# Small matmuls of a chunked recurrence issued in unbroken runs, with regrouped low-rank and first projections, in a two-layer decoder step on one core

## The chip, the core and the metric

The program runs on one core of a Trainium2 chip. The core has a matmul engine (TensorE, PE in the profile, with its weight loads shown as PEld), VectorE (DVE), ScalarE (ACT), GpSimd (POOL) and a queue for transfers (SP). Each engine takes its instructions in the order in which the program lists them. The metric is the device time of one execution in microseconds (us), the median of several runs.

## The reference

One inference step over two layers, for 1040 prompt tokens (16 learned ones ahead of 1024 given ones) and 8 single decode tokens, with width 1024. Layer 0 has a causal convolution module as its token mixer, layer 1 has RWKV-7 time mixing with 16 heads of 64; a squared-ReLU MLP of width 4096 follows each.

```python
def _wkv7_step(S, inp):                      # one token of the recurrence, per head
    r_t, w_t, k_t, v_t, kk_t, a_t = inp
    sa = jnp.einsum('bhvk,bhk->bhv', S, -kk_t)
    S = (S * w_t[:, :, None, :] + sa[..., None] * (kk_t * a_t)[:, :, None, :]
         + v_t[..., None] * k_t[:, :, None, :])
    y = jnp.einsum('bhvk,bhk->bhv', S, r_t)
    return S, y
...
    xx = prev - h                            # _rwkv7: six mixed inputs x? = h + xx * x_mix[?]
    r = (xr @ w_r).astype(f32)
    k = (xk @ w_k).astype(f32)
    v = (xv @ w_v).astype(f32)
    w_log = -jax.nn.softplus(-(w0 + jnp.tanh(xw @ w1) @ w2).astype(f32)) - 0.5
    decay = jnp.exp(-jnp.exp(w_log))
    a = jax.nn.sigmoid((a0 + (xa @ a1) @ a2).astype(f32))
    g = jax.nn.sigmoid(xg @ g1) @ g2
    kk = (k * k_k.astype(f32)).reshape(hs)
    kk = kk / jnp.maximum(jnp.sqrt(jnp.sum(kk * kk, axis=-1, keepdims=True)), L2_EPS)
    ...
    out = ((yn + bonus).astype(h.dtype) * g) @ w_o
```

## The kernel before

**Precision.** Every large product is three matmuls (`mm3`, L209 to L213): weight and activation are each split into a high and a low part (`_hi`/`_lo`, `_h`/`_l` or `mh`/`ml`), and high·high, low·high and high·low are summed in one PSUM bank. The splits are made by ACT (the high part, L177 or L159) and by POOL or DVE (the low part, L182 or L160).

**Stages in time.** Layer 0 runs first (three token groups of about 350). The mixer of layer 1 runs over four token groups of about 260 (`mixer_in(g)`); for each group it makes the eight `r` projections (`p_r`), the eight `k` projections (`p_k`) and the eight `v` projections (`p_v`), one per 128 output columns, each 24 matmuls. Before each of the three stands `mixed(i)`, which makes eight activation tiles (DVE L877, then the split). Beside them run the low-rank branches: `gate()` and `decay_rate()` call `narrow()`, 48 matmuls for one bank (`p_g`, `p_wa`), and the second stages `l_g`, `l_w`, `l_a` are three matmuls per 128 columns. The decay branch's result is split into `lwh`/`lwl` and `lah`/`lal`. `spread()` (`pb`, L804) spreads the key norms over the partitions, two matmuls into the one bank of pool `x`, read by DVE at L1157. `finish()` makes the blocks `nn` for the recurrence, sixteen matmuls of 64 x 32 per 128 columns. Last come the output projection (`ps_oo`) and the MLP of layer 1 (`ps_in`, `out`), for one token group and then for two.

**The recurrence** goes in 17 chunks of 64 tokens (`chunk(c)`), each prepared by `front(c)` (`A`, and the inverse of 32 x 32 blocks on DVE, L1232 and L1233). The chunk's products are small: `gg` and `po` are sixteen matmuls of 32 x 32 each, `W`, `U`, `S` sixteen of 64 columns each, `Y` 32. In the profile each of these shows as two records, as do all with f32 operands. They use only a part of the array (the profile prints the part, as 32\*32, 64\*64, 128\*64, 64\*32). One chunk is a chain: `W` needs the state `sv`; `U` needs `w1`, a copy of `W`, and `p64`, into which `po` is copied; `S` needs `uv`, a copy of `U`; the next state needs `S`.

**What sets the order.** The code is generators that a driver steps (`beside`, `filler`, `advance`), so that chunks, norm gates and MLP are traced interleaved. A list scheduler then orders each engine's instructions by readiness in its own estimate and by the place in the trace; `tc.high_priority(offset)` moves what it encloses up in that order. The eight banks of PSUM are shared in turn: in mixer groups 1 to 3, `mm` has four, `x` one and `w` (recurrence, transposes, `A`) three.

In the `r`, `k` and `v` stages the side generators are stepped by `beside(gen, places)`, at the calls whose number modulo 3 is in `places`.

Of the kernel before, what the change touches and what calls it, by code (L numbers as in the profile page):

```python
# [16 lines left out]
P = 128  # L17
# [31 lines left out]
def hybrid_step(tc, x_prompt, x_sample, state_conv, state_shift, state_wkv, meta_tokens,  # L49
# [10 lines left out]
    with ctx:  # L60
# [158 lines left out]
        def dense_steps(w, act, n, name):  # L219
            ps = bank(f"ps_{name}")  # L220
            for k in range(KT):
                mm3(ps[:, :n], (w[0][:, k, :], w[1][:, k, :]), (act[0][:, k, :n], act[1][:, k, :n]), k == 0, k == KT - 1)
                if k == KT // 2 - 1:
                    yield
            return ps
# [72 lines left out]
        def mlp_in(pl, hv, n, layer, name, sums):  # L298
# [3 lines left out]
            for k in range(KT):  # L302
                g = vec("norm_mlp", layer * KT + k)
                nc.scalar.activation(ah[:, k, :n], hv[:, k, :], AF.Copy, scale=g)  # L304
                nc.vector.scalar_tensor_tensor(al[:, k, :n], hv[:, k, :], g, ah[:, k, :n].bitcast(F32),
                                               op0=ALU.mult, op1=ALU.subtract)
# [25 lines left out]
        HEAD = 8  # L332
        STEPS = 2.6
# [80 lines left out]
        with ExitStack() as le:  # L414
# [76 lines left out]
            def transpose_x(g, ah, al):  # L491
# [19 lines left out]
                for k in range(KT):  # L511
# [4 lines left out]
                    nc.scalar.activation(ah[:, k, :n], ps[:, :n], AF.Copy, scale=gk)  # L516
                    nc.vector.scalar_tensor_tensor(al[:, k, :n], ps[:, :n], gk, ah[:, k, :n].bitcast(F32),
# [85 lines left out]
            def ln_silu(g):  # L603
# [14 lines left out]
                for k in range(KT):  # L618
# [4 lines left out]
                    split(ah[:, k, :n], al[:, k, :n], s[:, :n], nc.gpsimd)  # L623
# [208 lines left out]

        prep = {}
# [57 lines left out]
        def mixer_in(g, tick, ahead):  # L891
# [33 lines left out]

            nl = n if npr == n else npr + 2 * DEC
# [20 lines left out]
            def narrow(i, name):  # L947

                ps = bank(nm("p", name))[:, :nl]
                for hf in range(2):  # L950
                    w = load_w(d_lr[i, :, hf * HK:(hf + 1) * HK].rearrange("p k s c -> p (k s) c"), (KT, P), nm(name, hf), nc.gpsimd)
                    yield
                    for k in range(hf * HK, hf * HK + HK):
                        for s_ in range(2):
                            j = k % HK * 2 + s_
                            mm3(ps, (w[0][:, j, :], w[1][:, j, :]), [t[:, 1 - s_:1 - s_ + nl] for t in hxs[k]],
                                j == 0 and hf == 0, j == KT - 1 and hf == 1)
                        yield
# [15 lines left out]
            def gate():  # L974
                yield from input_parts()
# [31 lines left out]
            def beside(gen, places, slow=1.0):  # L1007
# [3 lines left out]
                def trace():  # L1011
                    tick(slow)
                    if calls[0] % 3 in places:
# [6 lines left out]
            aside = gate()  # L1020
            both = beside(aside, (0, 1))
            for p in range(KT):
                (both if p else lambda: tick(1.0))()
                ps = proj(next(wrkv), act, P, f"r{p}", both if p else lambda: tick(1.0))
                if p == 0:
                    carry["tail"]()
                r = t_("st", p, "em", 2)
# [42 lines left out]


            for _ in aside:
                pass
            act = mixed(3)
            both = beside(ahead, (1, 2), VSLOW)

            def finish(p, rk, ab, vv):
                def trace():
# [25 lines left out]
                    for c in range(ncg):  # L1104
                        for q in range(2):
                            for j in range(2):
                                o, js = 64 * q + 32 * j, slice(32 * j, 32 * j + 32)
                                nc.tensor.matmul(pn_[o:o + 32, c * 32:(c + 1) * 32], ab[HALF[q], c, 2, js], ab[HALF[q], c, 0, js],
                                                 start=True, stop=True, tile_position=(64 * q, o))
# [26 lines left out]
            for p, rk2 in ahead_of(fetch):  # L1136
# [18 lines left out]
                pb = bank(nm("pb", p), "x")  # L1155
# [140 lines left out]

        def chunk(c):
# [7 lines left out]
            def quads(name, pairs, lhs, rhs):  # L1305
                ps = bank(f"{name}{c}", "w")
                for p in range(KT):
                    for i, o in pairs:
                        nc.tensor.matmul(ps[Q[o], p * 32:(p + 1) * 32], lhs(i, p), rhs(i, p), start=True, stop=True,
                                         tile_position=(32 * i, 32 * o))  # L1310
                return ps, ps[:, :256].rearrange("p (k t) -> p k t", k=KT)
            down, up = [(0, 1), (2, 3)], [(1, 0), (3, 2)]

            ps, _ = quads("gg", down, lambda i, p: no[Q[i], p, :], lambda i, p: x32[Q[i], p, :])
            gg = w_([P, KT, 32], "gg", c, "x32")
            for i in (1, 3):
                nc.scalar.copy(flat(gg[Q[i]]), ps[Q[i], :256])
# [11 lines left out]
            for h in range(2):  # L1329
# [3 lines left out]
                nc.scalar.copy(flat(bkt[:, h * 4:h * 4 + 4]), ps)  # L1333
            yield RW[3]

            ps = bank(f"W{c}", "w")
            for p in range(KT):
                for q in range(2):
                    nc.tensor.matmul(ps[HALF[q], p * HS:(p + 1) * HS], xa[:, p, q, :HS], sv[:, p, q, :], start=True, stop=True)
# [371 lines left out]
```

## Time and profile before

| | us |
|---|---|
| median of 3 runs | 2870.38 (2868.0 to 2870.67) |
| the profiled execution | 2873.75 |
| its span, first to last instruction | 2872.0 |
| PE busy / PEld / DVE / ACT / POOL | 2708.4 / 2579.9 / 1986.7 / 1348.8 / 1627.1 |
| layer 0 alone, then beside the first mixer group | 0 to 898, 898 to 1245 |
| mixer groups 1 to 3 (with chunks 0 to 10) | 1245 to 1877 |
| output projection, first group, then MLP with chunks 12 to 16 | 1877 to 1924, 1924 to 2145 |
| rest of layer 1 | 2145 to 2872 |

A row of a view by windows gives a stretch, then for each engine its busy time and its number of instructions, then the granted PE clock (1.00 is full), the share of the transfer engines and GB/s. In a timeline a row has its start, its length, engine, line, operation, output and inputs, the part of the array, the size of the result and the number of records in a row. Matmuls are pipelined: the distance between two starts, not the length, is what one costs.

### The profile page before, as it was taken

The page shows a single profiled execution, that of the slowest core. Times are in us where ns is not written, and L with a number is a line of the kernel's source. Part 1 is how long each engine was busy: PE and PEld are TensorE (multiplying, and loading weights), DVE is VectorE, ACT ScalarE, POOL GpSimd, SP SyncE. Part 2 cuts the span into 40 slices and gives each one's busy share as a digit, 9 for nine tenths or more (in the row PEclk, how much of TensorE's full clock was granted, in tenths as well). Part 3 has the DMA queues.
Part 4 walks back from the last instruction along what each step waited for, and adds up shares of the span by engine and source line. Part 5 has one row for each costly group of instructions (what it writes and reads, how often), then busy time and mean ns, then how long its engine had stood idle before and what let it go on. Part 6 is the DMA issues. An engine that isn't in the chain of part 4 may idle for free. (4 is left out here: it accounts for less than half of the span.)

```text
span 2872.0 us, 54182 instructions
## 1 busy us (share of the span) xinstructions
PE 2708.4 (94%) x20554; PEld 2579.9 (90%) x20554; DVE 1986.7 (69%) x3752; ACT 1348.8 (47%) x2517; POOL 1627.1 (57%) x2191
## 2 busy tenths in 40 slices
PE   8999999999998999978888989989999999999998
PEld 7989999999998999978787778778789999999998
DVE  5999999995467455788886794674697664443444
ACT  5545444544354345555666755543344452222223
POOL 6687878987775454643444363454457783333332
PEclk9999999999999999989898989888999999999999
DMA  6572544454445555686778857865457642222211
GB/s 181 156 197 87 157 138 132 138 180 137 140 122 159 158 151 164 204 217 174 214 188 219 207 157 191 213 174 133 128 136 232 188 132 85 69 72 67 67 59 41
DMA packets 659283, 428.32 MB, mean 149 GB/s; under 512 B 126840, under 2 KB 609208, under 8 KB 659022
## 3 DMA queue, kind: packets, MB, share of 16 engines
q1 hardware_dynamic: 652780, 421.93, 52.4%
q8 instruction: 162, 2.65, 0.4%
q10 hardware_dynamic: 6018, 2.89, 0.4%
q14 instruction: 99, 0.81, 0.1%
q0 software_dynamic: 224, 0.03, 0.0%
HBM read 353.03 MB, written 72.66 MB: 148 GB/s over the span
## 5 line engine op out<-in xcount | busy, mean ns | idle before, releaser
L182 POOL TENSOR_TENSOR wo_lo<-wo_raw,wo_hi 128x256 fp32r<-128x256 f32 x672 | 517.1, 801 | 333.9 <-ACT wo_hi L177 287.5
L182 POOL TENSOR_TENSOR wi_lo<-wi_raw,wi_hi 128x256 fp32r<-128x256 f32 x600 | 462.7, 802 | 331.2 <-ACT wi_hi L177 318.3
L211 PE MATMUL out<-hh,wo_hi 128*128 128x352 f32 (+2 forms) x1536 | 503.7, 330 | 19.0 <-DVE h L382 8.2
L382 DVE TENSOR_TENSOR h<-h,out 128x352 f32<-128x352 f32 (+2 forms) x768 | 383.5, 510 | 195.5 <-PE out L213 195.1
L211 PE MATMUL ps_in<-m_h,wi_hi 128*128 128x352 f32 (+2 forms) x1536 | 499.5, 325 | 5.4 <-ACT m_h L304 3.7
L212 PE MATMUL out<-hh,wo_lo 128*128 128x352 f32 (+2 forms) x1536 | 500.8, 326 | 1.9 <-DVE wo_lo L182 1.9
L212 PE MATMUL ps_in<-m_h,wi_lo 128*128 128x352 f32 (+2 forms) x1536 | 498.0, 325 | 1.0 <-POOL wi_lo L182 0.8
L213 PE MATMUL ps_in<-m_l,wi_hi 128*128 128x352 f32 (+2 forms) x1536 | 498.3, 325 | 0.0
L213 PE MATMUL out<-hl,wo_hi 128*128 128x352 f32 (+2 forms) x1536 | 496.2, 326 | 1.6 <-DVE hl L160 1.6
L552 DVE SCALAR_TENSOR_TENSOR cv<-u,wdw,cv 128x352 f32<-128x352 f32 (+2 forms) x720 | 377.5, 575 | 0.7
L177 ACT CAST wo_hi<-wo_raw 128x1024 fp32r<-128x1024 f32 x184 | 192.7, 1049 | 328.4 <-PE ps_in L213 151.7
L177 ACT CAST wi_hi<-wi_raw 128x1024 fp32r<-128x1024 f32 x160 | 167.8, 1049 | 369.5 <-PE out L213 201.0
L211 PEld LDWEIGHTS out<-hh,wo_hi 128*128 128x128 f32 x1536 | 292.8, 191 | 27.3 <-DVE h L382 11.2
L211 PEld LDWEIGHTS ps_in<-m_h,wi_hi 128*128 128x128 f32 x1536 | 292.6, 191 | 8.4 <-ACT m_h L304 3.9
L212 PEld LDWEIGHTS out<-hh,wo_lo 128*128 128x128 f32 x1536 | 293.8, 191 | 4.7 <-DVE wo_lo L182 2.9
L213 PEld LDWEIGHTS out<-hl,wo_hi 128*128 128x128 f32 x1536 | 292.4, 191 | 3.4 <-DVE hl L160 2.1
L212 PEld LDWEIGHTS ps_in<-m_h,wi_lo 128*128 128x128 f32 x1536 | 292.1, 190 | 3.3 <-POOL wi_lo L182 1.8
L213 PEld LDWEIGHTS ps_in<-m_l,wi_hi 128*128 128x128 f32 x1536 | 291.5, 190 | 1.7
L369 DVE SCALAR_TENSOR_TENSOR r<-ps_in,rs_m 128x352 f32<-128x352 f32 (+2 forms) x192 | 98.5, 515 | 234.3 <-PE ps_in L213 230.5
L160 DVE TENSOR_TENSOR hl<-s,hh 128x352 fp32r<-128x352 f32 (+2 forms) x192 | 138.3, 721 | 97.7 <-ACT hh L159 97.4
L371 ACT ACTIVATE s<-r 128x352 f32<-128x352 f32 (+2 forms) x192 | 93.7, 491 | 138.0 <-DVE r L369 136.7
L182 POOL TENSOR_TENSOR wv_lo<-wv_raw,wv_hi 128x256 fp32r<-128x256 f32 x96 | 81.4, 878 | 44.0 <-ACT wv_hi L177 34.5
(408 smaller groups left out, 6251.9 us busy)
## 6 DMA issues: line engine op xcount, KB each, us to landing
wi_raw<-in_w_mlp_in_dram SPq DMA_DIRECT2D x160, 512.0 KB
wo_raw<-in_w_mlp_out_dram SPq DMA_DIRECT2D x160, 512.0 KB
wr_raw<-in_rwkv_w_r_dram SPq DMA_DIRECT2D x32, 512.0 KB
wk_raw<-in_rwkv_w_k_dram SPq DMA_DIRECT2D x32, 512.0 KB
wv_raw<-in_rwkv_w_v_dram SPq DMA_DIRECT2D x32, 512.0 KB
d_ab<-ab SPq DMA_DIRECT2D x32, 512.0 KB
pg_raw<-in_conv_w_pw_dram SPq DMA_DIRECT2D x24, 512.0 KB
pa_raw<-in_conv_w_pw_dram SPq DMA_DIRECT2D x24, 512.0 KB
```

The lines of the kernel that those rows point to most:

```text
L160: eng_lo.tensor_sub(lo, src, hi.bitcast(F32))
L177: nc.scalar.copy(hi[:, :a * b], raw[:, :a * b])
L182: eng_lo.tensor_sub(lo[:, cs], raw[:, cs], hi[:, cs].bitcast(F32))
L211: nc.tensor.matmul(ps, w[0], act[0], start=first, stop=False)
L212: nc.tensor.matmul(ps, w[1], act[0], start=False, stop=False)
L213: nc.tensor.matmul(ps, w[0], act[1], start=False, stop=last)
L369: nc.vector.scalar_tensor_tensor(r[:, :n], ps[:, :n], 0.0, rs[:, :n], op0=ALU.max, op1=ALU.mult)
L371: nc.scalar.activation(s[:, :n], r[:, :n], AF.Square)
L382: nc.vector.tensor_add(hv[:, 4 * i + m, :], hv[:, 4 * i + m, :], ps[:, :n])
L552: nc.vector.scalar_tensor_tensor(acc[m][:, :n], ug[:, m, j:j + n], wdw[:, m, j:j + 1], acc[m][:, :n], op0=ALU.mult, op1=ALU.add)
```

## The change

- `burst(lead, rest)` is new: it traces a list of matmuls at a priority raised by 400, and makes those in `rest` issue after the `lead` ones. `nn`, `gg`, `W` with `po`, `U`, and `S` with `Y` and the next chunk's `gg` are traced through it. `po` moves up to stand right behind `W`; `gg` of chunk c+1 moves into chunk c, behind `Y`, where the next front is done by then.
- `narrow()` loads both halves of its weights first and then issues its 48 matmuls with no step in between; `places` become lists of call numbers, so that `gate`'s matmuls come behind the last `r` projection and `decay_rate`'s behind the first `v` projection. `mixed(2)` and `mixed(3)` are traced ahead of the rest of the side generator.
- `pair()` is new: the first two `r` projections of a group alternate between two banks, tile by tile of the activation.
- `pb` takes a bank of `mm` for odd p.
- `new_act()` gives eight tiles instead of one of eight parts (its users index them).

```diff
         def new_act(pl, name, nmax, tag="act"):
-            return (pl.tile([P, KT, nmax], F32R, name=f"{name}_h", tag=f"{tag}h"),
-                    pl.tile([P, KT, nmax], F32R, name=f"{name}_l", tag=f"{tag}l"))
+            return tuple([pl.tile([P, nmax], F32R, name=f"{name}_{q}{k}", tag=f"{tag}{q}", bufs=KT) for k in range(KT)] for q in "hl")
...
+        BURST = 400
...
+        def burst(lead, rest):
+
+            with tc.high_priority(offset=BURST):
+                first = lead[0]()
+                for f in lead[1:]:
+                    with tc.issue_after(first.ins):
+                        nxt = f()
+                    first = nxt
+                with tc.issue_after(first.ins):
+                    for f in rest:
+                        f()
...
+            def pair(ws, act, names, fill):
+                banks = [bank(nm("p", x)) for x in names]
+                for k in range(KT):
+                    for ps, w in zip(banks, ws):
+                        mm3(ps[:, :n], (w[0][:, k, :], w[1][:, k, :]), act[k], k == 0, k == KT - 1)
+                    if k in (1, 3, 5):
+                        fill()
+                return banks
...
             def narrow(i, name):
 
+                ws = []
+                for hf in range(2):
+                    ws.append(load_w(d_lr[i, :, hf * HK:(hf + 1) * HK].rearrange("p k s c -> p (k s) c"), (KT, P), nm(name, hf), nc.gpsimd))
+                    yield
                 ps = bank(nm("p", name))[:, :nl]
-                for hf in range(2):
-                    w = load_w(...)
-                    yield
-                    for k in range(hf * HK, hf * HK + HK):
-                        for s_ in range(2):
-                            ...
-                        yield
+                for k in range(KT):
+                    w = ws[k // HK]
+                    for s_ in range(2):
+                        ...
                 return ps
...
-                    if calls[0] % 3 in places:
+                    if calls[0] in places:
...
+            act = mixed(2)
             for _ in aside:
                 pass
-            act = mixed(2)
             aside = decay_rate()
-            both = beside(aside, PL_K)
+            both = beside(aside, (3 * KT - 2, 3 * KT - 1))
...
-                pb = bank(nm("pb", p), "x")
+                pb = bank(nm("pb", p), "mm" if p % 2 else "x")
...
             ps = bank(f"W{c}", "w")
-            for p in range(KT):
-                for q in range(2):
-                    nc.tensor.matmul(ps[HALF[q], p * HS:(p + 1) * HS], xa[:, p, q, :HS], sv[:, p, q, :], start=True, stop=True)
+            po = bank(f"po{c}", "w")
...
+            burst(first[-2:], first[:-2] + up)
...
             ps = bank(f"S{c}", "w")
...
+            nxt = None
+            if c + 1 in chunks:
+                ggs[c + 1], mms, nxt = block_products(c + 1, chunks[c + 1][3], chunks[c + 1][5])
+                rest += mms
+            burst(ss[:2], rest)
```

Counted over PE's matmuls in program order, two neighbours have different tile sizes 627 times before and 352 times now. From the first `ps_in` of layer 1 to the last `pfs` (the final state's transpose) it is 246 times before and 70 now; the other 381 become 282. The order of PE up to the first `p_r` of group 0 is the same.

PE in the MLP of layer 1, chunk 13 (`W13`, `po13`: the chunk's small matmuls; `out1`: the MLP's second product; `yn`: a transpose of a norm gate), before:

```order
L1491 MATMUL yn5_1_24297<-ident_58,ey5_1_24142 128x96 x4
L1339 MATMUL W13_24384<-sv_14395,xa1_14402 64x64 x3
L211 MATMUL out1_2_0_2_24440<-hh10_4_23832,wo1_0_2_0_hi_24352 128x328
L1339 MATMUL W13_24384<-sv_14395,xa1_14402 64x64
L212 MATMUL out1_2_0_2_24440<-hh10_4_23832,wo1_0_2_0_lo_24353 128x328
L1339 MATMUL W13_24384<-sv_14395,xa1_14402 64x64
L213 MATMUL out1_2_0_2_24440<-hl10_4_23833,wo1_0_2_0_hi_24352 128x328
L1339 MATMUL W13_24384<-sv_14395,xa1_14402 64x64 x3
```

`W13` and, in the same way behind it, `po13` stood one by one between wide matmuls. Now, at the same place:

```order
L211 MATMUL out1_2_0_1_24602<-hh10_4_23998,wo1_0_2_0_hi_24521 128x328
L1527 MATMUL yn5_1_24466<-ident_58,ey5_1_24296 128x96 x4
L1369 MATMUL W13_24536<-sv_14521,xa1_14528 64x64 x16
L1321 MATMUL po13_24537<-p3213_24291,gg13_24394 32x32 x16
L212 MATMUL out1_2_0_1_24602<-hh10_4_23998,wo1_0_2_0_lo_24522 128x328
L213 MATMUL out1_2_0_1_24602<-hl10_4_23999,wo1_0_2_0_hi_24521 128x328
```

All sixteen of each now stand in a row.

PE at the start of group 2's `v` stage, behind the first `v` projection (`p2_v0`), before (`vt`: a transpose of `v`):

```order
L804 MATMUL pb2_0_18999<-r16h2_18879,hspread_10020 128x256
L1091 MATMUL vt2_0_19107<-ident_58,vv2_0_18997 128x128 x2
L804 MATMUL pb2_0_18999<-r16l2_18880,hspread_10020 128x256
L804 MATMUL pb2_1_19137<-r16h2_18879,hspread_10020 128x256
L804 MATMUL pb2_1_19137<-r16l2_18880,hspread_10020 128x256
L804 MATMUL pb2_2_19299<-r16h2_18879,hspread_10020 128x256
L804 MATMUL pb2_2_19299<-r16l2_18880,hspread_10020 128x256
```

Three spreads followed each other through one bank, and the decay branch (`p2_wa`) had been done in the `k` stage. Now the last rows of `p2_wa` stand here:

```order
L213 MATMUL p2_wa_19022<-hxl2_1_1_17656,wa2_1_hi_18939 128x256
L804 MATMUL pb2_0_19141<-r16h2_18966,hspread_10146 128x256
L804 MATMUL pb2_0_19141<-r16l2_18967,hspread_10146 128x256
L804 MATMUL pb2_2_19385<-r16h2_18966,hspread_10146 128x256
L804 MATMUL pb2_2_19385<-r16l2_18967,hspread_10146 128x256
L211 MATMUL l22_w0_19127<-lwh_10170,wa22_hi_19119 128x256
L212 MATMUL l22_w0_19127<-lwh_10170,wa22_lo_19120 128x256
L211 MATMUL l22_a0_19133<-lah_10172,wa22_hi_19119 128x256
```

The second stages `l22_w0` and `l22_a0`, which need the split result of `p2_wa`, now follow it after four matmuls.

More of the change, by code (lines that the diff above doesn't have):

```diff
@@ L1019, in mixer_in @@
             act = mixed(0)
-            aside = gate()
-            both = beside(aside, (0, 1))
+            aside = chain(input_parts(), gate())
+            both = beside(aside, [i for i in range(3 * KT) if i in (4, 6, 8, 10, 12) or i in (3 * KT - 3, 3 * KT - 2)])
             for p in range(KT):
-                (both if p else lambda: tick(1.0))()
-                ps = proj(next(wrkv), act, P, f"r{p}", both if p else lambda: tick(1.0))
+                both()
                 if p == 0:
+                    first = pair([next(wrkv), next(wrkv)], act, [f"r{i}" for i in range(2)], both)
                     carry["tail"]()
+                ps = first[p] if p < 2 else proj(next(wrkv), act, P, f"r{p}", both)
                 r = t_("st", p, "em", 2)
@@ L1069, in mixer_in @@
             norms()
+            act = mixed(3)
             for _ in aside:
                 pass
-            act = mixed(3)
-            both = beside(ahead, (1, 2), VSLOW)
+            both = beside(ahead, [i for i in range(3 * KT) if i % 3], VSLOW)
             def finish(p, rk, ab, vv):
@@ L1295, in hybrid_step, with quads, block_products, evict @@
         fronts = {}
+        ggs = {}
+        def quads(ps, pairs, lhs, rhs):
+            return [lambda p=p, i=i, o=o: nc.tensor.matmul(ps[Q[o], p * 32:(p + 1) * 32], lhs(i, p), rhs(i, p), start=True, stop=True,
+                                                           tile_position=(32 * i, 32 * o))
+                    for p in range(KT) for i, o in pairs]
+        def block_products(c, no, x32):
+            ps = bank(f"gg{c}", "w")
+            gg = w_([P, KT, 32], "gg", c, "x32")
+            def evict():
+                for i in (1, 3):
+                    nc.scalar.copy(flat(gg[Q[i]]), ps[Q[i], :256])
+            return gg, quads(ps, [(0, 1), (2, 3)], lambda i, p: no[Q[i], p, :], lambda i, p: x32[Q[i], p, :]), evict
         def chunk(c):
@@ L1303, in chunk @@
             sv, uv = st["sv"], st["uv"]
-            def quads(name, pairs, lhs, rhs):
-                ps = bank(f"{name}{c}", "w")
-                for p in range(KT):
[L1308 to L1317, printed above, removed]
+            gg = ggs.pop(c) if c in ggs else None
+            if gg is None:
+                gg, mms, evict = block_products(c, no, x32)
+                burst(mms[-2:], mms[:-2])
+                evict()
             p64 = w_([P, KT, HS], "p64", c)
@@ L1352, in chunk @@
             ps = bank(f"U{c}", "w")
-            for p in range(KT):
-                for q in range(2):
-                    nc.tensor.matmul(ps[HALF[q], p * HS:(p + 1) * HS], p64[HALF[q], p, :], w1[HALF[q], p, :], start=True, stop=True)
+            us = heads(ps, lambda p, q: p64[HALF[q], p, :], lambda p, q: w1[HALF[q], p, :])
+            burst(us[:2], us[2:])
             nc.vector.tensor_copy(uv[HALF[0], :, 0, :], kv(ps)[HALF[0]])
@@ L1379, in chunk @@
                     nc.sync.dma_start(d_y[t0:t0 + HS].rearrange("t (k q v) -> q t k v", q=2, v=HS)[q], yt[HALF[q]])
+            if nxt:
+                nxt()
             fs = w_([P, KT, HS], "fs", c, "w1")
@@ L1575, in mixer_out @@
                     nc.sync.dma_start(t[:, :n], d_z[:, p, lo:lo + n])
-                    split(z[0][:, p, :n], z[1][:, p, :n], t[:, :n], nc.vector)
+                    split(z[0][p][:, :n], z[1][p][:, :n], t[:, :n], nc.vector)
                 for m in range(KT):
```

58 lines of the change are left out of this document (29 added, 29 removed).

## The prediction

> **What bounds the kernel now.** I read the page first, then the busy time by stretches, then PE's timeline in the stretches that stand out, then the waits.
>
> ```profile
> span 2872.0 us, 54182 instructions
> PE 2708.4 (94%) x20554; PEld 2579.9 (90%) x20554; DVE 1986.7 (69%) x3752; ACT 1348.8 (47%) x2517; POOL 1627.1 (57%) x2191
> PEclk9999999999999999989898989888999999999999
> ```
>
> PE is busy 94% of the span, so it is the bound, and its granted clock falls only in the middle of the span. By stretches (the columns are stretch, length, busy time and records of PE, PEld, DVE, ACT, POOL, then clock, DMA share, GB/s):
>
> ```profile
> core 0: us, PE busy (x) PEld busy (x) DVE busy (x) ACT busy (x) POOL busy (x), PEclk, DMA share, GB/s
> 1245.00:1445.00 200.00, 166.44 (x1721) 148.35 (x1720) 164.10 (x329) 114.36 (x268) 83.00 (x121) 0.87 0.78 202
> 1445.00:1653.00 208.00, 177.86 (x2190) 159.39 (x2188) 156.17 (x306) 137.89 (x311) 85.24 (x106) 0.94 0.78 202
> 1653.00:1877.00 224.00, 204.73 (x2195) 179.25 (x2196) 150.72 (x292) 131.41 (x318) 111.90 (x181) 0.87 0.74 194
> 1924.00:2145.00 221.00, 215.30 (x2000) 180.71 (x2002) 150.78 (x311) 93.25 (x190) 108.03 (x132) 0.91 0.52 135
> 2145.00:2872.00 727.00, 709.56 (x4501) 702.50 (x4497) 371.15 (x665) 250.69 (x412) 358.17 (x461) 1.00 0.34 102
> ```
>
> The last row has no recurrence in it and runs at full clock. The row from 1924 to 2145 has the same MLP beside chunks 12 to 16: PE is as busy there, idle for only 5.7 of 221 us, at clock 0.91. So what it loses is lost while it is busy. The three mixer rows lose both ways: 83 us of idle time in 632, and clock.
>
> **The change of tile size.** PE's timeline in the MLP of layer 1 shows the loss: `po` (32 x 32 of the array) stands between wide matmuls one by one. The last two rows are the same wide matmuls undisturbed.
>
> ```profile
> 1977.15 0.41 PE L213 MATMUL ps_in<-m_l,wi_hi 128*128 128x328 f32 x1
> 1977.50 0.24 PE L1309 MATMUL po<-p,gg 32*32 32x32 f32 x2
> 1977.67 0.41 PE L211 MATMUL ps_in<-m_h,wi_hi 128*128 128x328 f32 x1
> 1985.08 0.31 PE L211 MATMUL ps_in<-m_h,wi_hi 128*128 128x328 f32 x1
> 1985.23 0.31 PE L212 MATMUL ps_in<-m_h,wi_lo 128*128 128x328 f32 x1
> ```
>
> From one wide start to the next are 0.52 us with `po` in between and 0.15 without. And this is the price round an unbroken run, in the mixer:
>
> ```profile
> 1602.94 0.28 PE L213 MATMUL p_v<-ml,wv_hi 128*128 128x256 f32 x1
> 1603.06 0.28 PE L211 MATMUL p_v<-mh,wv_hi 128*128 128x256 f32 x1
> 1603.27 1.15 PE L1355 MATMUL U<-w,p 64*64 64x64 f32 x32
> 1619.79 0.69 PE L1309 MATMUL po<-p,gg 32*32 32x32 f32 x32
> 1620.42 0.39 PE L213 MATMUL p_v<-ml,wv_hi 128*128 128x256 f32 x1
> L1309 PE MATMUL po<-p,gg 32*32 32x32 f32 x544 | 18.5, 196 | 0.0
> ```
>
> Into `U` are 0.21 us against 0.12 between two `p_v`: 0.09 for the change. The 32 `po` take 0.63 to the next start, 0.02 each; the last of them starts at 1619.79 + 0.69 - 0.20 = 1620.28, and 0.14 pass to the `p_v` against 0.02 within the run: 0.12. So a long run costs 0.09 + 0.12, about 0.10 a change; an alternation costs 0.52 - 0.15 - 0.04 (two `po`) = 0.33 a pair, 0.165 a change.
>
> **Term 1, changes removed.** In program order 176 fewer changes from the first `ps_in` to the last `pfs`, nearly all alternations: 176 x 0.165 = 29.0 us. Elsewhere 99 fewer, mixed; I take the lower price: 9.9 us. Together 39. The ends are all 275 at 0.10 (27) and all at 0.165 (45).
>
> **Term 2, the clock.** The half-clock stretches of this trace are multiples of 3.4 us. Some of them, and 3.4 us before some:
>
> ```profile
> 1957.60:1961.00 3.40, 3.40 (x21) 2.14 (x20) 0.70 (x2) 1.44 (x3) 0.00 (x0) 1.00 0.39 67
> 1961.10:1971.30 10.20, 10.20 (x49) 8.00 (x48) 1.96 (x5) 2.36 (x4) 2.79 (x4) 0.50 0.20 49
> 1974.70:1978.10 3.40, 3.40 (x21) 2.04 (x21) 0.44 (x2) 0.75 (x1) 3.00 (x5) 1.00 0.96 190
> 1978.10:1984.90 6.80, 6.80 (x27) 5.36 (x27) 0.45 (x1) 0.72 (x2) 0.26 (x1) 0.50 0.28 63
> 2029.30:2039.60 10.30, 10.30 (x41) 7.88 (x41) 2.43 (x5) 2.09 (x4) 0.58 (x1) 0.50 0.28 68
> 1763.10:1769.90 6.80, 6.80 (x29) 5.66 (x30) 1.26 (x2) 2.67 (x8) 2.02 (x3) 0.50 0.06 17
> 1595.80:1599.20 3.40, 3.40 (x69) 2.58 (x67) 0.50 (x1) 3.27 (x7) 0.46 (x1) 1.00 0.43 120
> 1599.20:1602.60 3.40, 3.40 (x73) 3.23 (x73) 1.96 (x6) 2.66 (x8) 3.34 (x6) 1.00 1.05 200
> ```
>
> The first and third row are alternations: PE is never idle in 3.40 us and the clock halves right after. The last two rows are nearly all small matmuls in runs (69 and 73 records), and the clock stays at 1.00. So the gate answers to how thin the work is, and changes thin it. The four half-clock rows sum to 34.1 us, half of which is lost: 17. I take 17; the ends are 0 (another cause closes the gate) and 25 (other half-clock stretches go too).
>
> [...]
>
> **Term 3, waits that are moved.**
>
> ```profile
> PE pb L804 <- DVE rk L1157: 9.9, 6, 3.7
> PE p_k L211 <- ACT mh L159: 4.7, 3, 1.9
> PE p_r L213 <- DVE ml L160: 4.5, 2, 3.7
> PE l_a L211 <- ACT wa L1146: 3.8, 2, 2.2
> PE S L1364 <- ACT uv L1357: 3.4, 1, 3.4
> 1541.03 0.40 ACT L159 CAST lwh<-lf 64x256 fp32r<-64x256 f32 x1
> 1541.96 1.60 POOL L160 TENSOR_TENSOR lwl<-lf,lwh 64x256 fp32r<-64x256 f32 x1
> 1543.64 0.73 POOL L160 TENSOR_TENSOR lal<-lf,lah 64x256 fp32r<-64x256 f32 x1
> ```
>
> `pair` and the early `mixed` aim at the second and third row: with two products per activation tile, or 48 low-rank matmuls (48 x 0.12 = 5.8 us) to run while tiles are made, I take most of it, 7 of 9.2. Two banks for `pb` aim at the first row, but `pb2_0` and `pb2_2` still follow each other in the `x` bank; I take 3 of 9.9. Against this, `l_w` and `l_a` now stand four matmuls behind `p_wa`: two ACT evacuations and two casts of about 0.40 each and POOL's 1.60 + 0.73 lie between, 3.9 us a group, and PE has half a microsecond of work for it. In group 0 the MLP covers it; in groups 1 to 3 it costs up to 11.7, where 3.8 was waited before. I take 5 more. `narrow` also holds two weight pairs of the ring at once, so the `w` stream's splits (DVE) may come late by one; I cost that at nothing, since the stream runs one split ahead. Net gain 5. Ends: 20 lost (the decay chain in full, late weights, bursts waiting) to 20 gained.
>
> **The rest.** `new_act` issues no instruction more or less. A freed tile would help where an activation is rewritten, as at the first MLP product of layer 1, but there the writer is not held by it:
>
> ```profile
> 1922.54 0.84 ACT L276 ACTIVATE sq<-h 128x328 f32<-128x328 f32 x2 [5.09 <-DVE acc_m L288]
> 1923.29 2.85 ACT L304 ACTIVATE m_h<-h,pvec 128x328 fp32r<-128x328 f32 x6
> ```
>
> ACT waits 5.09 us for DVE's sum, and `m_h` is queued behind. I count 0. `narrow` issues the same four weight loads, four ACT casts and sixteen POOL subtractions per group, closer together; POOL is busy 83 to 112 us in the mixer rows and SP's loads stay ahead of them, so I count 0 (without that room, the late-weight end of term 3).
>
> **Term 4, what does not come through.** In the first mixer row DVE is busy 164.10 of 200 us, and PE idles 33.6 us. There PE is not alone in setting the pace, so of the mixer's part (9.9 of term 1, and the 6.80 us row's half, 3.4, plus what follows it) I let about half, 7, come back as waiting. In the MLP row, DVE's 150.78 us would be 83% of the 182 us that remain after 39, no more than the 82% of that mixer row; I take nothing off there.
>
> The sum: 39 + 17 + 5 - 7 = 54 us off the profiled execution's 2873.75, so 2819.75. The profiled execution stands 3.4 above the median of the runs, 2870.38; against that, 2816.
>
> **The rivals.**
> - *DVE and the chains pace the MLP stretch as well* (for it: its 150.78 us; against: 5.7 us idle now). If 1924 to 2145 stops at 200 us, 75% DVE, 21 come off there and some 4 elsewhere: 2845.
> - *The gate closes for another reason.* Term 2 is 0: 2870.4 - 37 = 2833. [...]
> - *Shorter stalls feed on themselves.* The mixer's idle 83 us brings the half clock after it. If a third of that, 28 us, goes too: 2788.
> - *Bursts wait at the head of the queue: slower.* PE takes its list in order. A burst put early by an estimate waits for `uv`, `w1` or `sv`, and the wide matmuls behind it wait along. 17 chunks have `W`, `U`, `S`: 51 places. At 54/51, about 1.1 us more each, the gain is eaten; at 1.5 us it is 2870.4 + 22 = 2893. Against it: the row of `S` has one such wait, 3.4 us, in all 17 chunks, and the runs stand as far behind their producers as the first of them did before.
> - *Long runs of small matmuls close the gate* (the change does not do what it is meant to). `S`, `Y` and `gg` in a row are 128 records, over 3.40 us. Once a chunk, 6.80 us at half clock, 17 x 3.4 = 58: no change, 2874. The last two gate rows speak against it.
>
> **How the numbers follow.** Forecast 0.58 (its own range 2795 to 2835); DVE paces 0.15; another gate cause 0.10; more stalls go 0.07; bursts wait 0.07; runs close the gate 0.03. The range 2785 to 2856 leaves out the last two and half of the stalls case, 0.14. About 0.2%, 5.7 us, is what a measurement can tell from no change: faster 0.90, the same 0.04 (the gate case and the edge of others), slower 0.06.
>
> **What would show it.** In the profile after: the MLP beside chunks 12 to 16 takes 180 to 190 us instead of 221, clock 0.95 or more (terms 1 and 2); `W`, `po`, `U`, `S`, `Y` stand as x32 and x64 rows; waits of `p_r` and `p_k` for `mh`/`ml` nearly gone, and a new wait of `l_w` or `l_a` for `lwh` or `lwl` of 2 to 4 us a group (term 3). I am wrong if that stretch stays over 205 us, if its clock stays at 0.91, or if waits of `W`, `U`, `S` sum to over 20 us.

## The result, and the profile after

The changed kernel takes 2823.01 us (median of 4 runs, 2818.73 to 2827.55), 0.9838 of the time before, 95% interval 0.9816 to 0.9859. The forecast was 2816. (Beside the three runs of the kernel before that make its median, one more took 7932.67 us; it is left out.) The profiled execution has a span of 2823.1 us, 48.9 less than before. Its page:

```profile
span 2823.1 us, 54212 instructions
PE 2628.4 (93%) x20554; PEld 2536.2 (90%) x20554; DVE 1996.6 (71%) x3752; ACT 1350.0 (48%) x2516; POOL 1647.1 (58%) x2191
PEclk9999999999999999998899999989999999999999
```

PE has the same 20554 records and is busy 80 us less; the other engines' busy times have hardly moved. So the matmuls themselves take less time. By stretches, with the columns of the prediction's table (mixer groups 1 to 3, then the MLP from the first `ps_in` to the first `pfs`, then the rest):

```profile
core 0: us, PE busy (x) PEld busy (x) DVE busy (x) ACT busy (x) POOL busy (x), PEclk, DMA share, GB/s
1242.70:1444.60 201.90, 156.42 (x1624) 143.28 (x1622) 160.49 (x313) 106.87 (x244) 87.75 (x112) 0.85 0.73 189
1444.60:1657.40 212.80, 176.65 (x2266) 160.79 (x2265) 166.21 (x316) 139.66 (x320) 87.75 (x109) 0.94 0.78 203
1657.40:1860.30 202.90, 175.92 (x2180) 158.36 (x2180) 144.04 (x278) 130.99 (x312) 114.14 (x180) 0.94 0.80 213
1910.40:2080.60 170.20, 154.25 (x1783) 142.10 (x1784) 134.19 (x285) 83.19 (x169) 96.55 (x120) 0.96 0.61 152
2080.60:2823.00 742.40, 725.21 (x4573) 717.33 (x4573) 390.10 (x700) 254.09 (x417) 371.48 (x473) 0.99 0.34 103
```

The MLP row fell from 221 to 170.20 us and its clock rose from 0.91 to 0.96. Some 15 us of that is work that now lies behind the row, whose length grew from 727.00 to 742.40; so 35 us are gained there. To the last `pfs` instead of the first the stretch takes 175.30 us, where it took 221. The three mixer rows fell from 632 to 617.6 us, but PE's idle time in them (length less busy) rose from 83 to 108.6 us.

PE's timeline beside chunk 13 shows the change itself:

```profile
1979.14 1.15 PE L1369 MATMUL W<-sv,xa 128*64 128x64 f32 x32
1980.22 0.69 PE L1321 MATMUL po<-p,gg 32*32 32x32 f32 x32
1980.84 0.41 PE L212 MATMUL out<-hh,wo_lo 128*128 128x328 f32 x1
1981.10 0.31 PE L213 MATMUL out<-hl,wo_hi 128*128 128x328 f32 x1
```

`W` and `po` stand as two rows of 32 records and take 1.70 us from the first start to the wide matmul that follows. And PE's seven longest waits from 898 to 2110 us (total, times, longest), with those of `pb` and `S` from further down:

```profile
PE nn L1127 <- DVE ab L1210: 15.5, 7, 7.5
PE l_w L211 <- ACT lwh L159: 13.1, 3, 7.9
PE yn L1527 <- DVE ey L1523: 9.7, 3, 7.7
PE A L1294 <- DMA bk<-d_ab: 8.4, 4, 4.2
PE A L1294 <- DVE w L1375: 6.9, 2, 3.9
PE p_wa L211 <- ACT wa_hi L177: 6.7, 3, 4.5
PE pn L1067 <- ACT sq L1075: 6.6, 1, 6.6
PE pb L804 <- DVE rk L1178: 4.4, 2, 2.8
PE S L1369 <- DVE uv L1389: 2.7, 2, 1.5
```

`l_w` for `lwh` is new, and `pn` was at 0.4 before. `nn` for `ab` was 5.5 before (with 6.7 more for `mh`), `yn` 3.0, `A` for `bk` 3.8. `pb` went from 9.9 to 4.4, and the waits of `p_r` and `p_k` for `mh` and `ml` are gone from the list.

**The loss and gain by kind.** I took the distances between the starts of all matmuls from 897 us to the second group's output projection (1391 us long before, 1342 after). A distance at full clock and without a change of tile size gives the kind's own time; what is beyond it is put down to a gap (idle over 0.15 us), to a change of tile size, or to half clock.

| us | before | after | gain | forecast |
|---|---|---|---|---|
| changes of tile size (term 1) | 80.6 | 38.8 | 41.8 | 39 |
| of these in the MLP | 36.7 | 7.5 | 29.2 | 29.0 |
| half clock (term 2) | 70.4 | 48.6 | 21.8 | 17 |
| idle (terms 3 and 4) | 111.3 | 142.6 | -31.3 | -2 |
| matmuls' own time, small gaps | 1129.0 | 1112.3 | 16.7 | 0 |

The sum is 49.0 us against 54. Terms 1 and 2 together gave some more than forecast; but 31 us came back as waiting, and 17 us came from what I had not counted: matmuls, the small ones above all, that take less each in the changed kernel. From start to start, at full clock and without a gap or a change, a record of 64\*64 takes 35.2 ns on average before and 31.4 after, of 128\*64 33.1 and 30.5, of 32\*32 18.9 and 16.7, of the whole array 146.9 and 145.9.

How the first and third row share the time lost at half clock is a choice. The table puts to the clock what the matmuls' own time grows by. If half of all busy time at half clock is put there instead, the changes gain 28.3 us (22.2 in the MLP) and the clock 32.0. The two rows together are 60 to 64 us either way, against 56 forecast.

### The profile page after: what moved, and what is told of

Its sections match the earlier page's. It is cut to its first block, busy times and chain, and to the rows that moved or that the text cites. A ratio compares the mean times of both kernels' runs of the same rounds, so it can differ in the third digit from the quotient of the medians.

```text
span 2823.1 us, 54212 instructions
## 1 busy us (share of the span) xinstructions
PE 2628.4 (93%) x20554; PEld 2536.2 (90%) x20554; DVE 1996.6 (71%) x3752; ACT 1350.0 (48%) x2516; POOL 1647.1 (58%) x2191
## 5 line engine op out<-in xcount | busy, mean ns | idle before, releaser
L211 PE MATMUL out<-hh,wo_hi 128*128 128x352 f32 (+2 forms) x1536 | 501.3, 328 | 19.1 <-DVE h L382 12.2
L182 POOL TENSOR_TENSOR wv_lo<-wv_raw,wv_hi 128x256 fp32r<-128x256 f32 x96 | 80.2, 866 | 39.3 <-ACT wv_hi L177 33.1
```

The source lines that it names most:

```text
L182: eng_lo.tensor_sub(lo[:, cs], raw[:, cs], hi[:, cs].bitcast(F32))
L211: nc.tensor.matmul(ps, w[0], act[0], start=first, stop=False)
```

## The experiments

Theory: the gain is the unbroken runs, through fewer changes of tile size and the clock these cost, and the regrouped front of the mixer (pairs, low-rank runs, earlier activations, two banks) gives nothing. Rivals: the front carries part of the gain; or the new places of `po` and `gg` do.

**Runs alone, front alone.** One kernel is the changed one with the front put back, the other the kernel before with the new front.

```diff
 # runs alone: narrow() and places as before, no pair(), mixed(i) behind the rest, one bank
-                pb = bank(nm("pb", p), "mm" if p % 2 else "x")
+                pb = bank(nm("pb", p), "x")
 # front alone: W, po, U, S, Y, gg, nn as before, and
+            act = mixed(2)
             for _ in aside:
                 pass
-            act = mixed(2)
```

> The changed kernel with its front parts put back as before: low-rank first stages interleaved, no pairs, activations made after the low-rank run, norm spread in one bank. Its PE list has 335 changes of tile size (before 627, changed 352). Theory (the gain is the unbroken runs, and the front parts give nothing and cost their new waits): 2813 to 2828 us, 0.980 to 0.985 of before; the waits of p_k and p_r for mh/ml and of pb for rk are back (some 19 us), the 13 us of l_w for lwh are gone. Rival (the front parts carry a good part of the gain): 2835 us or more, 0.988 or above.

> The kernel before with the front parts alone: pairs, low-rank first stages in one run each, activations earlier, norm spread in two banks; W, po, U, S, Y, gg and nn stay as before. 644 changes of tile size in PE's list (before 627). Theory: 2862 to 2885 us, ratio 0.997 to 1.005; from the first ps_in of layer 1 to the last pfs still 215 to 225 us. Rival (front parts carry the gain): 2825 to 2850 us, ratio 0.985 to 0.993.

Runs alone: 2815.45 us, ratio 0.9814 (0.98 to 0.9827). Front alone: 2882.09 us, ratio 1.0029 (1.0006 to 1.0053). Both are as the theory has it: all of the gain is in the runs, and the front costs some 8 us on either base (the intervals of runs alone and of the changed kernel overlap a little here; with a second measurement of the changed kernel, below, they do not). Runs alone, in the mixer groups and from the first `ps_in` to the last `pfs`:

```profile
1253.40:1440.00 186.60, 151.71 (x1622) 138.31 (x1622) 157.91 (x317) 108.14 (x248) 84.21 (x112) 0.87 0.77 201
1440.00:1648.30 208.30, 174.42 (x2171) 158.38 (x2169) 157.78 (x303) 137.69 (x313) 81.16 (x107) 0.93 0.79 202
1648.30:1856.50 208.20, 177.38 (x2277) 160.09 (x2273) 150.32 (x287) 133.49 (x319) 117.90 (x182) 0.93 0.82 211
1913.00:2088.70 175.70, 162.76 (x1798) 149.35 (x1796) 147.60 (x319) 86.68 (x174) 101.97 (x121) 0.96 0.63 160
```

The MLP is as in the changed kernel (175.70 against 175.30 us); the mixer groups take 603.1 us instead of 617.6, with 100 us idle instead of 109. In exchange group 1 starts 11 us later (1253.4 instead of 1242.7) and the first output projection takes 6 us longer (56.5 instead of 50.1); behind the MLP 8 us are saved. One miss in front alone: I expected its MLP at 215 to 225 us, and it took 235, with 277 changes of tile size where the kernel before has 246. There the loss came with the order that the scheduler made, not with the mixer, so "8 us on either base" is one number with two causes.

**Written in order, but not held together.**

```diff
-            with tc.high_priority(offset=BURST):
-                first = lead[0]()
-                ...
+            for f in lead + rest:
+                f()
```

> The changed kernel in which a run is only written in its order and gets no priority and no hold behind its first matmul; po, gg and nn stay where the change put them. Its PE list has 682 changes of tile size, 269 before the first ps_oo (changed kernel: 268) and 413 behind it (changed: 84, before: 262). Theory (changes of tile size cost 0.165 us each, and clock): 329 more changes are 54 us, with clock 55 to 80, so 2878 to 2903 us, slower than before; the stretch from first ps_in to last pfs takes 225 to 250 us instead of 175. Rival (the place of po and gg made the gain, not the unbroken run): 2820 to 2840 us.

2886.39 us, ratio 1.0062 (1.005 to 1.0074): the rival is out, and the kernel is slower than before. Its MLP row, to the last `pfs`, and PE's timeline there:

```profile
1904.20:2154.90 250.70, 246.43 (x1986) 192.82 (x1987) 169.03 (x345) 91.51 (x184) 106.58 (x133) 0.86 0.46 121
1958.58 0.42 PE L212 MATMUL ps_in<-m_h,wi_lo 128*128 128x328 f32 x1
1958.93 0.24 PE L1314 MATMUL po<-p,gg 32*32 32x32 f32 x2
1959.11 0.42 PE L213 MATMUL ps_in<-m_l,wi_hi 128*128 128x328 f32 x1
```

`po` stands one by one again, 0.53 us from wide to wide. Counted as in the table above, from the first `ps_in` to the last `pfs`, there are 402 changes of tile size and 68 in the changed kernel, and they cost 69.8 and 7.5 us: 62.3 / 334 = 0.187 us each, where I took 0.165. Half clock costs 16.2 and 5.6 us. With half of the busy time at half clock put to the clock instead, the changes cost 52.3 and 7.4 us, 0.134 each. PE is idle for 4.3 us here and for 15.8 there: where alternation goes, some waiting that it covered comes out. Priority and hold were taken away together, so which of them does it is not shown.

**The price of a change by itself.** A block of matmuls on constant data, appended to the changed kernel, each held behind the one before.

```diff
+            parts = [[wide, q32, q32] * 60, [wide] * 60 + [q32] * 120, [wide, q128, q128] * 60, [wide, q64, q64] * 60,
+                     ([wide] * 4 + [q32] * 8) * 15]
+            for part in parts + parts[::-1]:
+                for f in [wide] * 60 + part:
+                    chained(f)
```

> The changed kernel with a block of matmuls appended behind its end, every one held behind the one before it, all on the same data, with nothing to wait for. Five parts, each ahead of it 60 wide matmuls (128 x 128, 328 columns): (1) 60 times one wide and two 32 x 32 ones, (2) 60 wide and then 120 of the 32 x 32 ones in a run, (3) 60 times one wide and two of the whole array with 32 columns, so interrupted without a change of tile size, (4) 60 times one wide and two 64 x 64 ones, (5) 15 times four wide and eight 32 x 32 ones; then the five in reverse order. Theory (a change of tile size costs 0.165 us in alternation, and thin stretches close the clock gate without idle time): at full clock part 1 has 0.52 us from wide to wide, 31 us in all, part 2 some 11 to 12 us, part 3 0.20 to 0.30 us from wide to wide, part 4 as part 1, part 5 about 1.0 us a turn, 16 us; the clock falls to 0.50 within parts 1 and 4 and stays at 1.00 in part 2 and in the 60 wide ones. Rivals: it is the interruption and not the tile size (part 3 then costs 0.45 or more from wide to wide); the gate answers to idle gaps alone (clock 1.00 in all parts).

The windows of part 1, of part 2 (its wide matmuls, then its run), and of parts 3, 4 and 5:

```profile
2829.85:2881.35 51.50, 51.50 (x302) 32.15 (x300) 0.00 (x0) 0.00 (x0) 0.00 (x0) 0.56 0.00 1
2893.10:2902.05 8.95, 8.95 (x61) 8.95 (x60) 0.00 (x0) 0.00 (x0) 0.00 (x0) 1.00 0.01 2
2902.29:2911.64 9.35, 9.35 (x242) 9.28 (x241) 0.00 (x0) 0.00 (x0) 0.00 (x0) 0.78 0.01 2
2921.82:2957.59 35.77, 35.77 (x302) 35.77 (x301) 0.00 (x0) 0.00 (x0) 0.00 (x0) 1.00 0.00 1
2966.48:3030.54 64.06, 64.06 (x302) 44.39 (x301) 0.00 (x0) 0.00 (x0) 0.00 (x0) 0.55 0.00 1
3041.29:3062.48 21.19, 21.19 (x303) 17.52 (x301) 0.00 (x0) 0.00 (x0) 0.00 (x0) 1.00 0.01 2
```

PE is busy for the whole of every window, and in parts 1 and 4 the clock falls to one half: the gate closes without idle time, so that rival is out. Part 1 from its start, at full clock:

```profile
2830.33 0.41 PE L1730 MATMUL pqw<-pq_h,pq_h 128*128 128x328 f32 x1
2830.67 0.31 PE L1731 MATMUL pqt<-ident 32*32 32x32 f32 x4
2830.91 0.42 PE L1730 MATMUL pqw<-pq_h,pq_h 128*128 128x328 f32 x1
```

A turn is 0.58 us. A wide matmul takes 8.95 / 59 = 0.15 by the second window, and a small record 0.032 in a row (four of them 0.13): that leaves 0.30 for two changes, 0.15 each, near the 0.165 of the prediction. (At half clock a turn is 0.92, a wide matmul 0.273 and a small record 0.053, which leaves 0.22 a change.) In part 5 a turn of four wide matmuls and sixteen small records takes 21.19 / 15 = 1.41 us; less 4 x 0.15 and 16 x 0.032 that is again 0.30. By position: 0.09 into the run, 0.02 at its first record, 0.09 out of it, and 0.10 more from the first wide matmul to the second (0.256 instead of 0.15). That last part I had left out of my 0.10 a change round a long run; it shows in the kernel too, in the two rows behind `po` above (1980.84 to 1981.10, 0.26). So in this block a change costs 0.15 in a run and in alternation alike, and what a run saves is their number.

Of my expected sums, parts 1, 2, 4 and 5 were missed. Part 1 takes 51.50 us where I had 31, because the clock is at one half from 6 us on, and part 4 64.06 for the same reason; part 2 takes 18.5 instead of 11 to 12, and its run, for which I had expected full clock, is granted 0.78; a small matmul takes 0.064 here against 0.04 in the kernel (there neighbours lie in different parts of the array, here in the same one; whether this makes the difference was not tried); and part 5's 21 us instead of 16 are mostly these slower small ones, the rest the price of 0.10 that should have been 0.15.

Part 3 I had wrong as well: 0.60 from wide to wide, as the rival "interruption" has it. But each record of its small matmuls takes 0.11 in a row (PEld is busy for all of the 35.77 us: four records of loads of the whole array take 0.56 in part 3, sixteen of 32 x 32 0.58 in part 5), so four of them and a wide one make 0.59 by themselves, and the interruption adds nothing that can be seen. That a price hides behind these loads is not excluded.

**The new wait of `l_w`.** The low-rank run `p_wa` is put ahead of `k6`.

```diff
-            both = beside(aside, (3 * KT - 2, 3 * KT - 1))
+            both = beside(aside, (16, 17, 18))
```

> The changed kernel with the decay's low-rank run, p_wa, in the k projections before k6 instead of behind the last one; 339 changes of tile size. Theory (l_w stands right behind the chain tanh, copy, splits and waits for it): l_w's 13.1 us for lwh fall under 3, p_wa's 6.7 for wa_hi fall, and the time is 2808 to 2817 us, 0.978 to 0.981. Rival (PE then waits for something else that is late at the same place, DVE's activations or norms): 2819 to 2827 us, with nn, pb or p_v waits grown by 8 us or more.

2822.86 us, ratio 0.9838 (0.9824 to 0.9853): no change, in the rival's range, though not by the waits that it names. The wait for `lwh` is gone from the list; of these rows `pn` and `yn` have grown (they were 6.6 and 9.7), and `nn`, which the rival named, has not (15.5):

```profile
PE nn L1127 <- DVE ab L1210: 15.1, 7, 5.6
PE pn L1067 <- ACT sq L1075: 14.4, 2, 7.9
PE yn L1527 <- DVE ey L1523: 13.8, 4, 7.0
```

PE's idle time in the three groups is 109.3 us, where it was 108.6. So the wait that I had forecast was there, and taking it away gained nothing. What it waited for shows in the timeline of ACT in the changed kernel, and of PE:

```profile
1365.49 1.04 ACT L177 CAST wa_hi<-wa_raw 128x1024 fp32r<-128x1024 f32 x1 [7.57 <-DMA wa_raw<-in_rwkv_a_dram]
1366.88 1.28 ACT L992 ACT_TABLE_LOAD   x1
1368.17 0.38 ACT L992 ACTIVATE lf<-p_wa 64x256 f32<-64x256 f32 x1
1368.96 0.40 ACT L159 CAST lwh<-lf 64x256 fp32r<-64x256 f32 x1
1369.42 0.58 PE L211 MATMUL l_w<-lwh,wa_hi 128*128 128x256 f32 x1 [7.93 <-ACT lwh L159]
```

The last `p_wa` had long been issued (1360.15). ACT's queue stood 7.57 us at a cast that waited for a transfer of weights, and `lf` and `lwh` are queued behind it. This is the longest of the three waits, 7.9 of 13.1 us, and in it the chain of evacuations and casts that I had priced at 3.9 us a group is the smaller part. In the next one, 4.6 us, two table loads of 1.28 us and a cast of other weights stand in ACT's queue before `lwh`. I had counted neither.

**Which half of the front.** The changed kernel again, the runs with pairs and two banks, and the runs with the low-rank runs.

```diff
 # pairs and banks: narrow(), its places and mixed(i) as before
+                    first = pair([next(wrkv), next(wrkv)], act, [f"r{i}" for i in range(2)], lambda: tick(1.0))
 # low-rank runs: the changed kernel without pair(), and
+                pb = bank(nm("pb", p), "x")
```

> The changed kernel once more, on the same chip as the next two: 2818 to 2828 us, ratio 0.982 to 0.986.

> The unbroken runs with two of the four front parts: pairs of first projections and the norm spread in two banks; the low-rank first stages stay interleaved and the activations behind them as in the kernel before. 328 changes of tile size. Theory (the front's loss lies in the low-rank runs with their late splits, pairs and banks give 2 to 5 us): 2808 to 2816 us, ratio 0.978 to 0.981. Rival (the loss lies in pairs or banks): 2819 to 2828 us. A third possibility, that neither half matters by itself: 2813 to 2819 us.

> The changed kernel without pairs and with the norm spread in one bank: unbroken runs, low-rank first stages in one run each, activations earlier. 322 changes of tile size. Theory (the loss lies in the low-rank runs): 2822 to 2832 us, ratio 0.983 to 0.987. Rival (the loss lies in pairs or banks): 2810 to 2818 us.

| | us | ratio (interval) |
|---|---|---|
| changed kernel again | 2826.62 | 0.9857 (0.9838 to 0.9876) |
| runs, pairs and banks | 2813.41 | 0.9809 (0.9793 to 0.9825) |
| runs, low-rank runs | 2818.5 | 0.9822 (0.9801 to 0.9842) |

The intervals of the first two don't meet: without the low-rank part the changed kernel is 13 us faster. The third lies between, and can't be told from either of the others, so whether pairs make the low-rank part worse stays open. Against the first measurement of the changed kernel, 2823.01, the difference is 10 us. The versions also differ in changes of tile size: 352 in the changed kernel, 335 with the runs alone, 328 with pairs and banks, 322 with the low-rank runs; 24 fewer are 3.6 us at 0.15. The earlier place of `mixed` was not run by itself. Pairs and banks can't be told from the runs alone either (0.9814).

**Late weights?** In ACT's waits from 1235 to 1870 us, the rows for transfers sum to 49 us before, 54 with the runs alone, 53 with pairs and banks, 63 with the low-rank runs, 85 in the changed kernel. The longest of the changed kernel, and the same three with pairs and banks:

```profile
ACT wk_hi L177 <- DMA wk_raw<-in_rwkv_w_k_dram: 12.6, 4, 6.8
ACT st L1051 <- DMA d_rk<-st: 11.5, 4, 6.7
ACT wa_hi L177 <- DMA wa_raw<-in_rwkv_a_dram: 10.6, 2, 7.6
```

```profile
ACT st L1051 <- DMA d_rk<-st: 8.5, 3, 5.8
ACT wa_hi L177 <- DMA wa_raw<-in_rwkv_a_dram: 2.6, 2, 2.5
ACT wk_hi L177 <- DMA wk_raw<-in_rwkv_w_k_dram: 0.6, 1, 0.6
```

The low-rank part now asks for its two weights in a row at the end of a stage, next to the second stage's weight and the stream's own. So I spaced these loads and left the runs:

```diff
-... i in (4, 6, 8, 10, 12) or i in (3 * KT - 3, 3 * KT - 2)])
+... i in (4, 6, 8, 10, 12) or i in (18, 21)])
-            both = beside(aside, (3 * KT - 2, 3 * KT - 1))
+            both = beside(aside, (18, 21))
```

> The changed kernel with the two weight loads of each low-rank run stepped at calls 18 and 21 of the stage (before: 21 and 22, and 22 and 23); the 48 matmuls stay in one run where the change put them. 299 changes of tile size. In mixer groups 1 to 3 of the changed kernel ACT waits some 85 us for transfers, 49 before and 54 with the front parts put back: 12.6 for wk_raw, 10.6 for the second-stage wa_raw, 7.7 for the first-stage wa_raw, 11.5 for st. Theory (the four or five loads in a row at a stage's end find a ring of three raw buffers, their casts block ACT's queue, and l_w, pn and nn wait behind it): ACT's waits for transfers fall to 65 or less, the time to 2809 to 2818 us, ratio 0.979 to 0.982. Rival (what costs is the run itself, not its loads): 2820 to 2828 us, ratio 0.983 to 0.986.

> The unbroken runs with pairs and two banks for the norm spread, once more, beside the kernel with spaced loads: 2809 to 2818 us, ratio 0.979 to 0.983; if it is 0.984 or above, the gain of that version over the changed kernel does not hold.

Spaced loads: 2818.65 us, ratio 0.9823 (0.9805 to 0.9841), and 74 us of ACT's waits for transfers; both fall short of the theory's bound, and the interval takes in both readings. Nor do the traces put the little that was gained to the loads: PE's idle time from 897 us to the second group's output projection is 143.5 us, as in the changed kernel (142.6), and there are 299 changes of tile size instead of 352, 8 us at 0.15. With pairs and banks that idle time is 133.5 us. Pairs and banks again: 2813.17 us, ratio 0.9809 (0.9791 to 0.9828), as the first time. Time and ACT's waits for transfers go together over the kernels with the runs that do all the work (53 to 57 us at 2813, 54 at 2815, 63, 70 and 74 at 2818 to 2819, 84 to 90 at 2823 to 2827), which fits late weights, but does not show that they are the cause.

**What paces the mixer.**

```diff
-                nc.vector.tensor_mul(o, ni[:, :j, j:j + 1]...)      # the inverse's two operations per j
-                nc.vector.tensor_add(ni[:, :j, j + 1:], ni[:, :j, j + 1:], o)
 # and, on the runs with pairs and banks:
-        LO_R = LO_K = lambda p: nc.vector
+        LO_R = LO_K = lambda p: nc.gpsimd if p % 2 else nc.vector
```

> The changed kernel without the multiplications and additions that invert the 32 x 32 blocks (the two DVE operations of the loop over j, 99 us of DVE in the last three groups of the mixer); the load and the store of the blocks stay. It tells what paces those groups, in which PE waits 108 us. Theory (DVE paces them: in PE's gaps there it is busy 83% of the time): 2740 to 2780 us, PE's idle time in the three groups down to 70 or less. Rival (PE's waits there come from chains through ACT and DMA that merely pass DVE): 2805 to 2823 us, idle time still 95 or more.

> The unbroken runs with pairs and two banks, and with every second low part of w_r and w_k made by POOL instead of DVE: some 29 us of DVE less in the last three groups, some 73 us of POOL more, which is busy under half of the time there. 321 changes of tile size. Theory (DVE paces the mixer): 2790 to 2806 us, ratio 0.972 to 0.978. Rival (POOL's 3.2 us a split against 1.3 make the weights late): 2813 to 2835 us, with waits of p_r and p_k for w_lo of 10 us or more.

Without the inverse: 2793.39 us, ratio 0.9749 (0.973 to 0.9767), between the two expectations. Its three groups:

```profile
1239.20:1431.60 192.40, 163.17 (x1884) 149.22 (x1881) 122.84 (x223) 119.57 (x278) 85.06 (x112) 0.92 0.86 214
1431.60:1631.30 199.70, 170.32 (x2017) 155.99 (x2017) 130.42 (x229) 126.75 (x290) 86.90 (x108) 0.90 0.79 202
1631.30:1836.00 204.70, 172.58 (x2170) 156.82 (x2168) 127.44 (x215) 130.82 (x313) 119.30 (x181) 0.94 0.80 211
```

DVE has 90 us less there than in the changed kernel, and PE is still idle for 90.7 us instead of 108.6. DVE is one of the paces, not the pace; and as leaving out the inverse also shortens the chain of a chunk's front, the run does not tell DVE's load from that chain. With splits moved to POOL: 2818.43 us, ratio 0.9831 (0.9813 to 0.9849), against 2813 for the same kernel without the move, in the rival's range, though not by its wait: `p_r` and `p_k` wait 4.1 us for `w_lo`. What holds the mixer's other 90 us stays open.

## Why the prediction was right, and where not

- **Term 1, changes removed: right in place, and in size as far as it can be counted.** 41.8 us against 39, in the MLP 29.2 against 29.0; by the other way of counting 28.3 and 22.2. The price in alternation, 0.165, came out at 0.15 in the appended block and at 0.187 (0.134 by the other way) in the kernel without the hold. The price round a long run, 0.10, was too low: 0.15, above. Outside the MLP, 9.9 us forecast came out at 12.6 or at 6.1, by the way of counting.
- **Term 2, clock: right in kind, too small if anything.** 21.8 or 32.0 us by the two ways of counting, against 17; time at half clock fell from 247.4 to 184.3 us over the whole span. The rival that the gate closes for another reason, so that term 2 is 0, is out: 0.56 is granted in a window where PE is busy 51.50 of 51.50 us. Idle time costs the clock here too. All three stretches of half clock that are left in the MLP row begin in or right behind a wait of PE: at 1910.38 (4.49 us), at 2016.20 (2.17) and at 2040.09 (2.72). For the second, the 3.4 us ahead of the fall and those behind it:

```profile
2012.79:2016.20 3.41, 1.24 (x8) 0.99 (x7) 3.28 (x11) 0.90 (x4) 0.00 (x0) 1.00 0.14 47
2016.20:2019.61 3.41, 3.41 (x11) 2.85 (x10) 3.32 (x10) 2.03 (x4) 0.34 (x1) 0.50 0.56 186
```

- **Term 3, moved waits: this step failed.** I put it at 5 us gained, with 20 lost as the far end; the front lost some 8 us. `pair` and the early activations did take away the waits of `p_r` and `p_k`, and two banks took half of `pb`'s; `l_w` got its wait, 13.1 us where I had up to 11.7. But PE's idle time is 142.6 us with the front and 134.6 with the runs alone. I had costed the weight loads standing closer together at nothing, because the stream runs one split ahead; in the runs, the low-rank part costs 10 to 13 us beside pairs and banks (3 us without them, not clear of the noise), with ACT waiting 36 us more for transfers than before. That these waits are its cause was not shown.
- **Term 4, waiting that comes back: too small, and the larger miss.** I took 7 us off in the mixer and nothing in the MLP. With the runs alone PE's idle time rose by 23 us, from 111.3 to 134.6; the mixer groups' share of it from 83 to 100 us. In the MLP row it rose from 5.7 to 15.95 us in the changed kernel. The rival that DVE and the chains pace the MLP had this much right; its 200 us for the stretch did not come.
- **What I had not counted** made up for half of the 31 us: 17 us of the matmuls' own time. That the time came out within 7 us of the forecast owes this much to luck: two misses of opposite sign.
- **The other rivals.** Bursts that wait at the head of the queue: `W` and `U` are not in the list, `S` waits 2.7 us in all, far from 54. The wait is at `nn`, which goes in runs too: 15.5 us, where it was 12.2. Long runs that close the gate: the clock of the MLP rose from 0.91 to 0.96, and no half clock begins during a run of `S`, `Y` and `gg` in one piece (128 records, 3.57 us) or within 4 us behind it, so not at this length. More stalls go: they grew.
- **What was to be seen.** The rows of 32 and the clock are there, and the MLP's row was 170 us where I said 180 to 190, since some of its work went behind it.

## What to carry to other kernels

Small matmuls that use a part of the array belong in one run between wide ones: a change of tile size cost 0.13 to 0.19 us here by the way of counting, 0.15 in the block at full clock, and where single wide matmuls alternated with them, half the clock (0.56 granted over the 51.50 us of part 1). It takes a hold in the scheduler and not only the order in which they are written; written in order alone they made the kernel slower than before. Before work is gathered into runs elsewhere, look at what its loads are gathered next to: here a cast that waits 7.57 us for weights held up ACT's queue, and the version without that part (runs, pairs, two banks: 2813 us, 0.9809) beats both kernels, though not the runs alone (2815 us, 0.9814) by more than the noise.

## What the hardware showed that I had not expected

- In these traces the granted clock goes with the share of the time that matmuls of the whole array take, not with PE being busy nor with columns alone. Wide matmuls at 0.15 us: with one in a turn of 0.58 us with 32 x 32 ones (26% of the time) or of 0.69 us with 64 x 64 ones (22%) it falls to one half after some 6 us (0.56 and 0.55 over parts 1 and 4), and with 0.15 of 0.52 us (29%) in the kernel before it falls as well (0.50 from 1961.10 us on); with four in a turn of 1.41 us (43%) it stays at 1.00, and so it does in part 3, which streams the same number of columns as part 1 in nearly the same time (0.60 us a turn against 0.58 at full clock), but all of them through the whole array. For wide matmuls between small tiles the border lies between 29% and 43% here. Part 3 does not tell whole-array matmuls from their weight loads, which fill its window (PEld busy 35.77 of 35.77 us), so with which of the two the clock goes is not shown.
- A run of 32 x 32 matmuls alone brings the half clock too: the window of 9.35 us has a clock of 0.78, at one half from 5.3 us on, and in the second turn of the block from 3.5 us on (0.66 over 10.60 us). The run of `S`, `Y` and `gg` in the changed kernel (128 records) takes 3.57 us to the next wide matmul where nothing interrupts it. My rival of long runs was wrong by length, not by mechanism, and not by much.
- With the splits on POOL, 32 of DVE's went away, 39.6 us of them, but DVE's busy time fell by 13 (1987.9 to 1974.9). Its other operations, the same in both kernels, took 29 us longer in sum; between the two runs of the kernel with DVE's splits that sum differs by 0.1. The activations' mix of one shape, from 898 to 1870 us, with DVE's splits and then with POOL's:

```profile
L889 DVE SCALAR_TENSOR_TENSOR mx<-xx,pvec,hx 128x256 f32<-128x256 f32 x48 | 29.0, 621 | 0.4 <-POOL ml L160 0.2
```

```profile
L889 DVE SCALAR_TENSOR_TENSOR mx<-xx,pvec,hx 128x256 f32<-128x256 f32 x48 | 32.3, 696 | 1.6 <-POOL ml L160 1.5
```

  Why DVE slows while POOL is busier was not tried.
